# A hybrid encoder on one Trainium2 core: another order inside the block of seven products

## The chip, the cores and the metric

The kernel runs on one core of one Trainium2 chip. The metric is the device time of one execution in microseconds (us), and lower is better. The core has a matrix engine (TensorE, in the profile PE, with its weight loads as PEld), three engines for element work (VectorE or DVE, ScalarE or ACT, GpSimd or POOL) and a queue, SP, from which nearly all transfers between HBM and the core's memory are issued.

## The reference

Two layers work on 256 tokens of width 1024 in float32. Each has a token mixer and a gated MLP. The change touches the MLP alone:

```python
def _conv_ffn(xn, w_up, conv_w, conv_b, w_down):
    a, gval = jnp.split(xn @ w_up, 2, axis=-1)
    a = lax.conv_general_dilated(a, conv_w[:, None, :], ...,
                                 feature_group_count=D_FF) + conv_b
    return (jax.nn.gelu(a) * gval) @ w_down
```

D_FF is 2816, so `w_up` is 1024 x 5632 and `w_down` 2816 x 1024. The convolution takes each channel with its two neighbours in time.

## The kernel before

**Weights in pieces.** All weights stream through one object, `Weights`. A load (L174, on SP) brings 1 MB of float32 into a buffer `raw`; three such buffers take turns. (A load with a tag goes to a place of its own that is idle at the time.) Each load is used as two pieces, its halves 0 and 1. Each piece is split into two parts that TensorE takes at a higher rate: the high part `wh`, a copy by ScalarE (L255, here "the split"), and the low part `wl`, the remainder by VectorE (L257, "the rest"). Five pairs of `wh` and `wl` exist. A product then takes three matmuls for one of plain float32: x high by `wh`, x high by `wl`, x low by `wh`.

`get` (L278) hands the next piece to TensorE's code and, inside the MLP, splits the piece four further on. Behind that piece's rest comes whatever difference of weights `W.sums` holds for the piece (L224). Then `load` issues the loads that `ahead` (L148) names: as many as three untagged ones, from the earliest that is still needed by the piece just split and the two behind it.

**The order of the MLP is written by hand** (`manual_schedule`). Each piece has a place, counted from the start of the MLP, and the engines work in the order in which the code issues. `MLP_GROUPS` (L43) gives the groups: `a` and `g` with a number n are 512 columns of the convolved and of the gated half of `w_up`, four pieces of 12 matmuls each; `b` holds the last 256 columns of both halves; `w` is the block of seven products, which stands for columns group 3 of both halves; `d` are pieces of `w_down`, 12 matmuls each. a2 has places 16 to 19, g2 20 to 23, the block 24 to 45, b 46 to 49, a4 50 to 53, g4 54 to 57, and the rest are down pieces.

`at_place` (L1524) does what belongs to a place: the split of the piece four on (ACT), then whatever the place has "between" (VectorE's steps of a chunk, and the copies, additions and transposes that follow a finished group), then the rest of that piece (VectorE), then the matmuls, then what it has "behind". A finished group leaves TensorE's banks through two transposes on VectorE (L803), a write to HBM (L808) and four reads (L815), so that channels come to lie on partitions. This is called a crossing. The reads wait until the next load has been issued. All crossings of the MLP are transposed into one buffer, `crossing`.

**Chunk pairs.** The channels come in 22 chunks of 128, worked off in pairs f = 0, 2, ... 20. A pair has five steps (L1470): `fetch_up`, six scalings on ACT (L1486, L1488); `neighbours`, two additions on VectorE (L1492, L1493); `activate`, the gelu on ACT (L1496); `gate`, a multiplication on VectorE (L1500); and `keep_up`, a copy on ACT (L1508) and a subtraction on VectorE (L1509). `PAIR_PLACES` (L48) has two places p1 and p3 for each pair: `fetch_up` is behind p1, `neighbours` between and `activate` behind p1 + 1, `gate` between and `keep_up` behind p3. Chunks 8 and 9 need a2 and g2, chunks 12 to 15 the block, 16 to 19 a4 and g4, and 20 and 21 need b. Down piece k needs chunk k.

**The block** (L323 for the weights, L1550 for the products) computes two 512-column groups for even and odd tokens with seven products rather than eight. The weights' quadrants are "11" and "21" (upper and lower rows of the gated columns) and "12" and "22" (of the convolved ones). The products multiply "11", T1, "22", T2, "21", T3 and T4 by quadrants of x or by sums of them, where T1 = 12 - 11, T2 = 22 - T1, T3 = 22 - 12 and T4 = 21 - T2. Each difference is taken on VectorE in halves (L343), and each half is then split like any other piece. A half product has 6 matmuls. "11" and "12" are loaded to tagged places; "22" and "21" to `raw`. In before T1, T2 and T4 are written over "11" and T3 over "12".

`BLOCK` (L52) is the order of half products and down pieces ("d"), and `SUMS` (L57) says behind which piece each half of a difference is taken. The products share three banks: "11" and "21" one, T1 and "22" another, T2, T3 and T4 the third. Before a bank is added to further, its interim sum is taken out: "11" is copied to the third bank (L1592), T1 and "22" are copied out by ACT (L1596, L1599), and T2 and T3 are added to those copies by VectorE (L1603) and sent on their crossing.

Of the kernel before, what the change touches and what calls it, by code (L numbers as in the profile page):

```python
# [16 lines left out]
P = 128  # L17
# [28 lines left out]
)  # L46

PAIR_PLACES = (  # L48
    (11, 14), (14, 16), (19, 22), (21, 23), (46, 48), (49, 51), (52, 54), (58, 60), (61, 63), (64, 66), (66, 68),
)  # L50

BLOCK = (  # L52
    ("11", 0), ("11", 1), "d", ("T1", 0), ("T1", 1), "d", ("22", 0), ("22", 1), "d", ("T2", 0), ("T2", 1), "d",
    ("21", 0), ("21", 1), "d", ("T3", 0), ("T3", 1), "d", "d", ("T4", 0), ("T4", 1), "d",
)

SUMS = {  # L57
    ("11", 1): ("T1", 0), ("d", 0): ("T1", 1), ("22", 1): ("T2", 0), ("d", 2): ("T2", 1),
    ("T2", 0): ("T3", 0), ("T2", 1): ("T3", 1), ("21", 1): ("T4", 0), ("d", 4): ("T4", 1),
}  # L60
HALVES = (slice(0, 512), slice(512, D))
SEGMENTS = (HALVES, (slice(0, 512), slice(512, 768), slice(768, D)))

# [229 lines left out]
def encoder(ctx, tc, x, w_in, w_pool, pool_scale, w_a, w_b, w_o, norm1, norm2, w_up, conv_w,  # L293
            conv_b, w_down, rel_bias, norm_f, onehot, edges, out):
    nc = tc.nc
# [9 lines left out]
    W = Weights(tc, wpool, big, sm)  # L305

    def rows(w, r0, n=2, c0=0, width=1024, tag=None, pieces=2):

        src = w[r0 : r0 + n * P, c0 : c0 + width].rearrange("(k p) c -> p k c", p=P)
        h = n // pieces  # L310
        return W.add(
            src, (n, width), [((lambda t, j=j: t[:, j * h : (j + 1) * h, :]), (h, width)) for j in range(pieces)],
            tag,
        )
# [8 lines left out]
    def block(w, down, n):  # L323

        def quadrant(k, c0, tag=None):
            return rows(w, k * 512, 4, c0, 512, tag)

        gate, act = DFF + n * 512, n * 512
        made = {"11": quadrant(0, gate, "ybig"), "12": quadrant(0, act, "at2")}
        d = rows(down, 0)  # L330
        made["22"] = quadrant(1, act)
        d += rows(down, 2 * P)
        made["21"] = quadrant(1, gate)
        d += rows(down, 4 * P) + rows(down, 6 * P)
        home = {"T1": "11", "T2": "11", "T3": "12", "T4": "11"}
        of = {"T1": "12", "T2": "22", "T3": "22", "T4": "21"}

        def raw(name, j):
            return W.raw[made[name][0][0]][:, 2 * j : 2 * j + 2]

        def sum_of(name, j):
            at = raw(home[name], j)
            nc.vector.tensor_sub(out=at, in0=raw(of[name], j), in1=at)  # L343

        k = 0
        for unit in BLOCK:
            if unit == "d":
                key, piece = ("d", k), d[k]
                k += 1
            else:  # L350
                key = name, j = unit
                if name in home:
                    n0 = made["22"][0][0] if name == "T2" else d[k][0]
                    piece = (n0, lambda t, name=name, j=j: raw(home[name], j), (2, 512))
                else:
                    piece = made[name][j]
            if key in SUMS:
                W.sums[len(W.pieces)] = lambda name=SUMS[key]: sum_of(*name)
            W.use([piece])

    first_up = []
    for l in range(DEPTH):
# [8 lines left out]
        for kind, n in GROUPS:  # L371
            c0 = {"u": 0, "q": C_Q, "k": C_K}[kind] + n * 512
            pieces = rows(w_in[l], 0, 4, c0, 512)
            if (kind, n) in POOLS:
                g, at = POOLS[kind, n]
# [646 lines left out]
    for l in range(DEPTH):  # L1022
# [311 lines left out]
        with tc.manual_schedule():  # L1334
# [28 lines left out]
            for n, cc in enumerate(HALVES):  # L1363
# [14 lines left out]
                for t in range(2):  # L1378
                    nc.vector.scalar_tensor_tensor(
                        out=th[:, t], in0=th[:, t], scalar=1.0, in1=ps[t], op0=ALU.add, op1=ALU.mult  # L1380
# [12 lines left out]
            for i in range(4):  # L1393
                next(attended)
                if i >= 2:
                    made = first[i - 2][1]()
# [138 lines left out]
        def begin_values():  # L1535
# [7 lines left out]
        down = residual_mm(  # L1543
            lambda k: acts[k], NF, lambda *a: late["norm"].add(*a),
            fill=begin_values if l + 1 < DEPTH else None, whole=(l + 1 == DEPTH),
        )
# [130 lines left out]
```

## Time and profile before

| | us |
|---|---|
| median of 3 runs | 856.58 |
| lowest and highest of them | 855.93, 856.83 |
| the profiled execution as a whole | 859.7 |
| its span, first to last instruction | 857.9 |
| layer 1's block on TensorE | 312.50 to 356.07 |
| layer 2's block on TensorE | 734.55 to 778.73 |

Rows of a timeline give the start, the duration, the engine, the line and operation, what is written and read, how many instructions were merged, and in brackets how long the engine had been idle and what ended that. Durations overlap where instructions are pipelined, so the cost of an operation in a full queue is the distance from its start to the next one's. Rows of the chain of work that ended last give start, duration and what the end waited for. Rows by windows give, for a stretch, its length, the busy time of PE, PEld, DVE, ACT and POOL with the number of instructions, the clock granted to TensorE, the busy share of the DMA engines and GB/s.

### The profile page before, as it was taken

To read this page: it belongs to the slowest core of one execution; us is meant where nothing else is said; L and a number is where in the kernel's file an instruction comes from. 1 tells how busy PE (TensorE), PEld (TensorE's weight loads), DVE (VectorE), ACT (ScalarE), POOL (GpSimd) and SP (SyncE) were. 2 spreads that over 40 slices of the span, in tenths; PEclk is the share of its full clock that TensorE was granted. 3 is DMA by queue.
4 is the path that set the end of the run, shared out by engine and by line. 5 is a ranking of instruction groups with operands and counts; after the bars stand their busy time and mean duration, and the time that the engine had idled before them with its cause. 6 is when DMAs were issued, how large, how long until landed. Compare 5 with 4: busy or idle time off the path is not lost.

```text
span 857.9 us, 10949 instructions
## 1 busy us (share of the span) xinstructions
PE 841.6 (98%) x3901; PEld 700.7 (82%) x3901; DVE 646.1 (75%) x838; ACT 524.0 (61%) x757; POOL 35.6 (4%) x96
## 2 busy tenths in 40 slices
PE   9999999999999999999999999999999999899996
PEld 7888888888888887788788888888888888788885
DVE  6968777767767799787855787768577867987774
ACT  6744556654555775577745455577354657656784
POOL 1720000000010000000000000000000100000000
PEclk9999999999999999999999999999999999999998
DMA  8699986795748986798626889878776489758951
GB/s 300 210 309 306 299 283 226 263 294 210 249 163 291 284 289 214 234 325 281 239 99 221 263 280 322 247 228 266 247 260 240 147 271 322 265 197 280 333 171 50
DMA packets 147967, 214.03 MB, mean 249 GB/s; under 512 B 7800, under 2 KB 69184, under 8 KB 147912
## 3 DMA queue, kind: packets, MB, share of 16 engines
q1 hardware_dynamic: 147480, 212.67, 75.2%
q8 instruction: 31, 0.51, 0.2%
q10 hardware_dynamic: 432, 0.66, 0.2%
q14 instruction: 24, 0.20, 0.1%
HBM read 186.02 MB, written 27.28 MB: 249 GB/s over the span
## 4 chain that ended last, share of the span: by engine, by line
PE 79%; DVE 10%; DMA 7%; issue 2%; ACT 1%; SPq 1%; POOL 0%; ACTq 0%; DVEq 0%; POOLq 0%
PE t_ps L749 51%; PE v_ps L749 6%; DVE wl L257 5%; PE res_ps L667 5%; PE res_ps L668 5%; PE res_ps L666 5%; DMA raw<-in_w_down_dram 4%; PE v_ps L1002 3%; DMA crossing<-crossing 2%; DVE raw L343 2%; PE pool_ps L653 1%; PE v_ps L901 1%; DVE crossing L803 1%; PE o_ps L1285 1%; PE s_ps L1237 1%
## 5 line engine op out<-in xcount | busy, mean ns | idle before, releaser
L257 DVE TENSOR_TENSOR wl<-raw,wh 128x1024 fp32r<-128x1024 f32 x286 | 343.6, 1217 | 117.2 <-ACT wh L255 116.1
L255 ACT CAST wh<-raw 128x1024 fp32r<-128x1024 f32 x286 | 296.8, 1049 | 186.1 <-PE t_ps L749 98.4
L749 PE MATMUL t_ps<-wh,x 128*128 128x512 f32 x1280 | 399.8, 390 | 0.0
L749 PEld LDWEIGHTS t_ps<-wh,x 128*128 128x128 f32 x1280 | 240.3, 188 | 50.1
L749 PE MATMUL t_ps<-wl,x 128*128 128x512 f32 x640 | 249.0, 389 | 0.0
L749 PEld LDWEIGHTS t_ps<-wl,x 128*128 128x128 f32 x640 | 120.2, 188 | 24.7
L667 PE MATMUL res_ps<-wl,actq 128*128 128x512 f32 (+1 forms) x184 | 70.1, 381 | 1.1 <-DVE wl L257 1.1
L666 PE MATMUL res_ps<-wh,actq 128*128 128x512 f32 (+1 forms) x184 | 70.0, 380 | 0.0
L668 PE MATMUL res_ps<-wh,actk 128*128 128x512 f32 (+1 forms) x184 | 69.0, 380 | 0.0
L667 PEld LDWEIGHTS res_ps<-wl,actq 128*128 128x128 f32 x184 | 34.6, 188 | 8.5 <-DVE wl L257 1.9
L749 PE MATMUL t_ps<-wh,po 128*128 128x512 f32 x128 | 41.4, 395 | 0.0
L666 PEld LDWEIGHTS res_ps<-wh,actq 128*128 128x128 f32 x184 | 34.6, 188 | 6.7
L668 PEld LDWEIGHTS res_ps<-wh,actk 128*128 128x128 f32 x184 | 34.6, 188 | 6.5
L1488 ACT ACTIVATE a<-zga,prm 128x256 f32<-128x256 f32 x80 | 38.9, 513 | 0.0
L543 POOL TENSOR_SCALAR ss<-ss 128x1 f32<-128x1 f32 x8 | 2.3, 291 | 777.4 <-ACT junk L536 777.3
L803 DVE STREAM_TRANSPOSE crossing<-t_ps 128x512 f32<-128x512 f32 x36 | 23.9, 694 | 6.6 <-DMA crossing<-crossing 6.6
L749 PEld LDWEIGHTS t_ps<-wh,po 128*128 128x128 f32 x128 | 24.0, 188 | 4.9
L666 PE MATMUL res_ps<-wh,m 128*128 128x512 f32 (+1 forms) x72 | 26.5, 368 | 0.0
L667 PE MATMUL res_ps<-wl,m 128*128 128x512 f32 (+1 forms) x72 | 26.3, 365 | 0.0
L668 PE MATMUL res_ps<-wh,m 128*128 128x512 f32 (+1 forms) x72 | 26.0, 365 | 0.0
L749 PE MATMUL v_ps<-wh,x 128*128 128x512 f32 x80 | 25.7, 392 | 0.0
L749 PE MATMUL t_ps<-wl,po 128*128 128x512 f32 x64 | 24.9, 390 | 0.0
(211 smaller groups left out, 1045.5 us busy)
## 6 DMA issues: line engine op xcount, KB each, us to landing
raw<-in_w_in_dram SPq DMA_DIRECT2D x58, 1024.0 KB
raw<-in_w_up_dram SPq DMA_DIRECT2D x40, 1024.0 KB
raw<-in_w_down_dram SPq DMA_DIRECT2D x22, 1024.0 KB
crossing<-crossing SPq DMA_DIRECT2D x22, 512.0 KB
crossing<-way SPq DMA_DIRECT2D x16, 512.0 KB
raw<-in_w_a_dram SPq DMA_DIRECT2D x8, 1024.0 KB
raw<-in_w_o_dram SPq DMA_DIRECT2D x8, 1024.0 KB
zga<-crossing SPq DMA_DIRECT2D x40, 128.0 KB
```

Of the source, the lines that this page charges most:

```text
L255: inst = nc.scalar.copy(out=h, in_=src)
L257: inst = self.rests[i] = nc.vector.tensor_sub(out=l, in0=src, in1=h.bitcast(F32))
L343: nc.vector.tensor_sub(out=at, in0=raw(of[name], j), in1=at)
L653: nc.tensor.matmul(out, w(k), x, start=(steps is first and k == 0), stop=(steps is last and k == nk - 1), skip_group_check=turns["rest"],)
L666: nc.tensor.matmul(ps, ah, wh, start=first, stop=False, skip_group_check=on)
L667: nc.tensor.matmul(ps, ah, wl, start=False, stop=False, skip_group_check=on)
L668: nc.tensor.matmul(ps, al, wh, start=False, stop=last, skip_group_check=on)
L749: nc.tensor.matmul(ps, x2[:, 2 * n + j, part, t, :], w[:, j, :], start=(n + m == 0), stop=(n == last and m == 5),)
L803: nc.vector.transpose(out=y.rearrange("p q c j -> p c q j"), in_=rows)
L901: return nc.tensor.matmul(ps[t], a[:, k, t, :], w[:, k % 2, :], start=first, stop=last)
L1002: nc.tensor.matmul(ps[t], a[:, k, t, :], w[:, j, :], start=(k + m == 0), stop=(k == KD - 1 and m == 2),)
L1488: nc.scalar.mul(out=out, in_=a, mul=row(j, c))
```

## The change

- T1's two halves are taken behind the rests of the two pieces ahead of the block (g2's third and fourth). The halves of T2 are taken behind the rests of "22", T3's behind those of T2, T4's behind those of "21".
- T1, T2 and T4 are now written over "12", and T3, as T2 - 11, over "11". T3 no longer reads "22".
- Two down pieces stand ahead of "22" rather than one, and one ahead of T4 rather than two. The second down load is issued ahead of "22" and the third ahead of "21".
- The pairs from chunk 8 on have other places. Chunk 8's are 39 and 41, inside the block, rather than 46 and 48 behind it.

```diff
@@ -46,18 +46,15 @@
 )
 
 PAIR_PLACES = (
-    (11, 14), (14, 16), (19, 22), (21, 23), (46, 48), (49, 51), (52, 54), (58, 60), (61, 63), (64, 66), (66, 68),
+    (11, 14), (14, 16), (19, 22), (21, 23), (39, 41), (46, 48), (49, 51), (52, 54), (60, 62), (63, 65), (58, 60),
 )
 
 BLOCK = (
-    ("11", 0), ("11", 1), "d", ("T1", 0), ("T1", 1), "d", ("22", 0), ("22", 1), "d", ("T2", 0), ("T2", 1), "d",
-    ("21", 0), ("21", 1), "d", ("T3", 0), ("T3", 1), "d", "d", ("T4", 0), ("T4", 1), "d",
+    ("11", 0), ("11", 1), "d", ("T1", 0), ("T1", 1), "d", "d", ("22", 0), ("22", 1), "d", ("T2", 0), ("T2", 1), "d",
+    ("21", 0), ("21", 1), "d", ("T3", 0), ("T3", 1), "d", ("T4", 0), ("T4", 1), "d",
 )
 
-SUMS = {
-    ("11", 1): ("T1", 0), ("d", 0): ("T1", 1), ("22", 1): ("T2", 0), ("d", 2): ("T2", 1),
-    ("T2", 0): ("T3", 0), ("T2", 1): ("T3", 1), ("21", 1): ("T4", 0), ("d", 4): ("T4", 1),
-}
+SUMS = {"22": "T2", "T2": "T3", "21": "T4"}
 HALVES = (slice(0, 512), slice(512, D))
 SEGMENTS = (HALVES, (slice(0, 512), slice(512, 768), slice(768, D)))
 
@@ -327,36 +324,40 @@
 
         gate, act = DFF + n * 512, n * 512
         made = {"11": quadrant(0, gate, "ybig"), "12": quadrant(0, act, "at2")}
-        d = rows(down, 0)
+        d = rows(down, 0) + rows(down, 2 * P)
         made["22"] = quadrant(1, act)
-        d += rows(down, 2 * P)
+        d += rows(down, 4 * P)
         made["21"] = quadrant(1, gate)
-        d += rows(down, 4 * P) + rows(down, 6 * P)
-        home = {"T1": "11", "T2": "11", "T3": "12", "T4": "11"}
-        of = {"T1": "12", "T2": "22", "T3": "22", "T4": "21"}
+        d += rows(down, 6 * P)
+        made.update(T1=made["12"], T2=made["12"], T3=made["11"], T4=made["12"])
+        terms = {"T1": ("12", "11"), "T2": ("22", "12"), "T3": ("12", "11"), "T4": ("21", "12")}
 
         def raw(name, j):
             return W.raw[made[name][0][0]][:, 2 * j : 2 * j + 2]
 
-        def sum_of(name, j):
-            at = raw(home[name], j)
-            nc.vector.tensor_sub(out=at, in0=raw(of[name], j), in1=at)
-
+        def sum_later(i, name, j):
+
+            def make():
+                one, other = terms[name]
+                nc.vector.tensor_sub(out=raw(name, j), in0=raw(one, j), in1=raw(other, j))
+
+            W.sums[i] = make
+
+        for j in range(2):
+            sum_later(len(W.pieces) - 2 + j, "T1", j)
         k = 0
         for unit in BLOCK:
             if unit == "d":
-                key, piece = ("d", k), d[k]
+                W.use([d[k]])
                 k += 1
+                continue
+            name, j = unit
+            if name in SUMS:
+                sum_later(len(W.pieces), SUMS[name], j)
+            if name in terms:
+                W.use([(d[k][0], lambda t, name=name, j=j: raw(name, j), (2, 512))])
             else:
-                key = name, j = unit
-                if name in home:
-                    n0 = made["22"][0][0] if name == "T2" else d[k][0]
-                    piece = (n0, lambda t, name=name, j=j: raw(home[name], j), (2, 512))
-                else:
-                    piece = made[name][j]
-            if key in SUMS:
-                W.sums[len(W.pieces)] = lambda name=SUMS[key]: sum_of(*name)
-            W.use([piece])
+                W.use([made[name][j]])
 
     first_up = []
     for l in range(DEPTH):
```

## The prediction

> **What bounds the kernel now.** I read the cores view first, then the page, the chain of work that ended last, and the timelines of TensorE (PE), VectorE (DVE), ScalarE (ACT) and the SP queue through the block.
>
> ```profile
> core 0: 857.9 us, clock 0.997
> ```
> ```profile
> PE 841.6 (98%) x3901; PEld 700.7 (82%) x3901; DVE 646.1 (75%) x838; ACT 524.0 (61%) x757; POOL 35.6 (4%) x96
> ```
> ```profile
> 258.26 40.81 PE t_ps L749 x180
> ```
>
> TensorE is the bound, at full clock. The third line is from the chain: 180 matmuls without a gap in 40.81 us, 0.2267 us each. A block of seven products has just as many: 14 half products of 6 and 8 down pieces of 12. Without a wait it would take 40.8 us. The first PE rows of the block and of the piece behind it say what it does take, in layer 1 and layer 2:
>
> ```profile
> 312.50 0.39 PE L1578 MATMUL t_ps<-wh,x 128*128 128x512 f32 x1
> ...
> 356.07 0.39 PE L749 MATMUL t_ps<-wh,x 128*128 128x512 f32 x1
> ```
> ```profile
> 734.55 0.39 PE L1578 MATMUL t_ps<-wh,x 128*128 128x512 f32 x1
> ...
> 748.16 0.50 PE L1578 MATMUL t_ps<-wh,sx 128*128 128x512 f32 x1 [2.02 <-ACT kept L1596]
> ...
> 778.73 0.39 PE L749 MATMUL t_ps<-wh,x 128*128 128x512 f32 x1
> ```
>
> That is 43.57 and 44.18 us: 2.77 and 3.38 us lost, **6.15 us in all, the most that an edit inside the blocks can win**. The largest loss is the one shown: the third product ("22") opens on the bank that ScalarE still has to copy out (L1596), and that copy stands behind a split that waits for a difference.
>
> In the block the tight engine is VectorE. A half product is 6 × 0.2267 = 1.36 us on PE, but a half of a difference costs VectorE a rest (L257) and a subtraction (L343). Its rows around the entry of layer 1's block:
>
> ```profile
> 297.47 1.22 DVE L257 TENSOR_TENSOR wl<-raw,wh 128x1024 fp32r<-128x1024 f32 x1 [0.56 <-ACT wh L255]
> 300.19 1.23 DVE L257 TENSOR_TENSOR wl<-raw,wh 128x1024 fp32r<-128x1024 f32 x1 [1.50 <-ACT wh L255]
> 301.33 1.31 DVE L803 STREAM_TRANSPOSE crossing<-t_ps 128x512 f32<-128x512 f32 x2
> 302.56 0.65 DVE L1492 TENSOR_TENSOR y<-y,a 128x510 f32<-128x510 f32 x1
> 303.31 0.69 DVE L1493 TENSOR_TENSOR y<-y,a 128x510 f32<-128x510 f32 x1
> 303.96 1.23 DVE L257 TENSOR_TENSOR wl<-raw,wh 128x1024 fp32r<-128x1024 f32 x1
> 305.64 1.23 DVE L257 TENSOR_TENSOR wl<-raw,wh 128x1024 fp32r<-128x1024 f32 x1 [0.45 <-ACT wh L255]
> 307.37 1.23 DVE L343 TENSOR_TENSOR raw<-raw,raw 128x1024 f32<-128x1024 f32 x1 [0.51 <-DMA raw<-in_w_up_dram]
> ...
> 310.90 1.22 DVE L257 TENSOR_TENSOR wl<-raw,wh 128x1024 fp32r<-128x1024 f32 x1 [0.30 <-ACT wh L255]
> 312.04 1.22 DVE L343 TENSOR_TENSOR raw<-raw,raw 128x1024 f32<-128x1024 f32 x1
> 313.18 0.68 DVE L1509 TENSOR_TENSOR actk<-g,actq 128x512 fp32r<-128x512 f32 x1
> 313.78 0.68 DVE L1500 TENSOR_TENSOR g<-y,zg 128x512 f32<-128x512 f32 x1
> 314.38 1.22 DVE L257 TENSOR_TENSOR wl<-raw,wh 128x1024 fp32r<-128x1024 f32 x1
> ```
>
> From start to start: a rest 1.14 us, a difference 1.14, two transposes 1.23, a chunk pair's neighbours (L1492, L1493) 1.40, its keep (L1509) 0.60, its gate (L1500) 0.60. In program order the rows are the rests of g2's last two pieces (297.47 and 300.19), a2's transposes, neighbours of chunk 4, the rests of both halves of "11", and then T1's first difference at 307.37, which **waited 0.51 us for the load of quadrant "12"**. That load was issued late, behind others on SP:
>
> ```profile
> 298.94 0.40 SPq L174 DMA_DIRECT2D raw<-in_w_up_dram  x1
> ```
> ```profile
> 299.43 10.30 DMA raw<-in_w_down_dram
> ```
> ```profile
> 329.95 4.77 DMA raw<-in_w_down_dram
> ```
>
> It landed at about 307.3, 8.4 us after its issue. The next load, by the chain, was issued at 299.43 and landed at 309.73; the chain's shorter flight of a megabyte is 4.77 us.
>
> **The change part by part.**
>
> *T1's differences.* They move from behind the rests of "11" half 1 and down piece 0 to behind the rests of g2's last two pieces, three places earlier. Nothing in the diff issues "12" earlier: "11", "12" and the first down load are still issued once g2's first piece is split. So VectorE, which takes its queue in order, reaches the difference at 297.47 + 1.22 = 298.7 and stands there until 307.37: **8.7 us of waiting where 0.5 was**. Queued behind it are the rest at 300.19 and all rows up to 305.64; ACT waits behind them for the neighbours, PE for the rests. That work cost nothing before, under the flight of "12"; now it is behind it. Layer 2 has the same picture, with "12" landing just ahead of
>
> ```profile
> 730.65 1.22 DVE L343 TENSOR_TENSOR raw<-raw,raw 128x1024 f32<-128x1024 f32 x1 [0.61 <-DMA raw<-in_w_up_dram]
> ```
>
> 3.90 us ahead of PE's entry (734.55), where layer 1 has 5.13. Call the start of this first difference L. I count VectorE from L to the rest of T1's second half, the piece that PE reaches soonest relative to its rest. Two differences and six rests: 8 × 1.14 = 9.12; two pairs of transposes (a2, g2) 2.46; two neighbours 2.80; two gates and two keeps 2.40: 16.8 us. To that come two handoffs through ACT, from these rows:
>
> ```profile
> 304.04 0.64 ACT L1496 ACTIVATE y<-y 128x512 f32<-128x512 f32 x1
> 304.57 1.03 ACT L255 CAST wh<-raw 128x1024 fp32r<-128x1024 f32 x1
> 305.51 0.52 ACT L1488 ACTIVATE a<-zga,prm 128x256 f32<-128x256 f32 x1
> ...
> 307.74 0.51 ACT L1488 ACTIVATE a<-zga,prm 128x256 f32<-128x256 f32 x1
> ```
>
> Chunk 4's activation (0.53) follows its neighbours, the split of "11" half 1 (0.94) follows that, and chunk 6's six scalings (305.51 to 308.25, 2.74) follow that. These 4.2 us and VectorE's return (0.1) stand against 2 × 1.14 of rests and a gate of 0.60 that VectorE can do meanwhile: 1.4 us more, and 0.1 until the last rest is written. So that rest ends at L + 18.3 = 325.7. PE, unhindered, would want it at 312.50 + 3 × 1.36 + 2.72 + 0.23 = 319.5: **PE is 6.1 us late here in layer 1, and 7.4 in layer 2**.
>
> *Down pieces 1 and 2 ahead of "22".* PE then has 5.4 us rather than 2.7 between T1 and the bank that L1596 empties, so that wait goes; I count its gain within the sum. In return T3 and T4, which share a bank, have one down piece between them rather than two, so T4 must wait for VectorE's addition of T3 (L1603). "22", no longer read by T3's difference, frees its buffer a little earlier, which nothing in this sum waits for.
>
> *The loads' order on SP.* The second down load goes out where "22" did, and "22" one place later, behind a2's crossing, whose transposes now end at L + 3.4 + 1.2 = 312.0. With 4.8 us of flight it lands at 317; its split is wanted after T1's and d1's, past 325. That cover of 8 us hides it, and d1's rest frees the third down load's buffer at L + 19.4 = 326.8, to land at 331.6, with its split wanted past 336.
>
> *Chunk 8's steps into the block* (39, 41 for 46, 48): neighbours, gate and keep, 2.60 us, now stand on VectorE ahead of that addition. At 46 they were hidden. From the rest of T1's second half to the end of T3's addition VectorE has 17 rests (19.38), six differences (6.84), the first addition and transpose and the second addition, by
>
> ```profile
> 346.31 0.68 DVE L1603 TENSOR_TENSOR kept<-t_ps,kept 128x512 f32<-128x512 f32 x1
> 347.03 0.71 DVE L803 STREAM_TRANSPOSE crossing<-kept 128x512 f32<-128x512 f32 x1
> 351.52 0.72 DVE L803 STREAM_TRANSPOSE crossing<-t_ps 128x512 f32<-128x512 f32 x1 [3.79 <-DMA crossing<-crossing]
> 352.16 4.59 DVE L257 TENSOR_TENSOR wl<-raw,wh 128x1024 fp32r<-128x1024 f32 x4
> ```
>
> 0.72 + 0.64 + 0.72 = 2.08, and the 2.60: 30.9 us. **T4 can start at L + 18.3 + 30.9 = L + 49.2**: 356.6 in layer 1 and 779.9 in layer 2. PE, 6.1 and 7.4 late, would be there at 354.0 and 777.3 (312.50 or 734.55, plus 12 × 1.36 + 7 × 2.72 = 35.36): a second wait of some 2.5 us. T4 and the last down piece add 5.44: the blocks end at 362.0 and 785.3, against 356.07 and 778.73: **5.9 + 6.6 us**.
>
> *The first piece of b.* Its rest now stands behind T3's addition, a transpose, the 3.79 us for the crossing (the buffer of the two transposes is one) and another transpose, which in before delayed the last down piece. 356.6 + 0.64 + 3.8 + 0.64 + 1.2 = 362.9 against 362.2 needed (one matmul into the piece): **0.7 us** in each layer.
>
> *The other chunks* (10 to 20 at other places) lie where PE has no gap and ACT and DVE have room:
>
> ```profile
> 400.00:410.00 10.00, 10.00 (x45) 8.26 (x45) 7.68 (x11) 9.34 (x16) 0.00 (x0) 1.00 0.83 309
> ```
>
> Cost between 0 and, if ACT's 0.66 us of room were all used up, about 1 us a layer; gain at most nothing, since nothing waits. I take 0.
>
> **Sum:** 5.9 + 6.6 + 2 × 0.7 = 13.9 us on the profiled span: 871.8 for 857.9. That execution took 859.7 as a whole, 3.1 above the median of 856.58; I add the difference to the median: **870.5 us**.
>
> Two costs no row shows. *When "12" lands* with VectorE standing still: not before its issue plus the shortest flight, 298.94 + 4.77 = 303.7, so L is up to 3.7 us earlier and the whole up to 7.4 lower, 863.1; I stay by 307.37, as nothing ahead of it in the queue changes. *Quadrant "21"*: it can be loaded only when d3's rest frees its buffer, about L + 26.3, and its split is wanted 4.6 us later. A flight of 4.77 just serves; one of 8.4, as that of "12", would idle VectorE for 3.8 us more a layer, 878.1 in all. DMA is light there, so I go by the short one.
>
> **The rivals.**
>
> 1. *The flight of "12" shrinks* (863 to 867). For it: later loads and a2's write compete less. Against: the load behind it landed 2.4 us later, as if each had its turn. The Trainium skill ("DMA: Bandwidth & Descriptors", Queues, rings and completion order) says that each DMA engine consumes descriptors in ring order, but that completion isn't first in, first out; by that rule later loads take nothing from "12"'s start, and this rival would be worth little.
> 2. *"21" or another late load adds a third wait* (874 to 878), with the bound worked out above.
> 3. *The other side, faster:* the load of "12" isn't what the difference meets, and only the two waits that the edit removes count. If VectorE reached the difference with "12" there, T4 could start at 298.7 + 49.2 = 347.9, the unhindered 347.86, plus some 1.5 us of VectorE's waits for splits: 42.3 + 0.7 us for the block and its follower where 43.57 were. With the same lead in layer 2 its 44.18 become 43.0 too: 1.8 us off the two, 854.8. It turns from loss to gain where "12" lands at 307.37 - 6.6 = 300.8, 1.8 us after its issue; the shortest flight is 4.77. I see no way to it but a misread order of the queues.
> 4. *The clock falls in the new waits.* The row with layer 2's 2.02 us wait shows full clock (the 1.00):
>
> ```profile
> 740.00:750.00 10.00, 7.76 (x33) 5.88 (x33) 10.00 (x11) 6.44 (x9) 0.00 (x0) 1.00 0.79 234
> ```
>
> A fall before T4 is swallowed by T4's wait; at half clock through T4 it costs 12 × 0.2267 = 2.7 us a layer: 876. The Trainium skill ("TensorE: Matmul & The Clock Gate", What's actually happening) has the clock halved after an idle window of about 3.4 us. By that rule none of my waits, 2 to 3 us each, would do it, though one somewhat longer would.
>
> **How the numbers follow.** My forecast (867 to 874): 0.62. Rival 1: 0.13. Rival 2: 0.13. Rival 3: 0.06, of which 0.04 beyond 0.2%. Rival 4: 0.06. The range goes from rival 1's lowest, 863.1, less 1.1 should the waits at b shrink with it, to the bound of "21", 878; outside it are rival 3 and what I have not thought of, which I put at 0.15 to 0.2 together. Slower by over 0.2% (1.7 us, about what a measurement can tell from no change): 0.62 + 0.13 + 0.13 + 0.06 = 0.94; faster 0.04; same 0.02.
>
> **What would show it.** Right: in the waits, "DVE raw <- DMA" grows from 1.1 to some 17 us in two waits of 8 to 9; the rest of g2's last piece starts at 308.5 rather than 300.2; PE waits at "11", at down piece 0 and at T1 for rests, and at T4 for L1603; the wait for L1596 is gone. Wrong: if the first difference waits little, rival 3 stands; if PE is late at T1 but not at T4, the count of chunk 8 is too high; if ACT waits for a load of w_up at "21", it is rival 2.

## The result and the profile after

The change makes the kernel slower: **863.16 us** against 856.25 us for the kernel before on the same chip (medians; 862.88 to 865.09 and 855.29 to 856.83), a ratio of 1.0087 with a 95% interval of 1.0069 to 1.0104. The prediction was 870.5 with a range of 862 to 878: the right side, inside the range, about twice the size.

The profiled execution took 863.14 us, close to its kernel's median, while that of before (859.7) stood 3.4 us above its own. The profiles therefore differ by only 3.4 us of span where the medians differ by 6.9. Sums below are made on the spans, as in the prediction, and sizes of single edits come from medians. Lines after L254 are those of before moved by a few: L252 is the split, L254 the rest, L342 a difference, L750 a matmul of an ordinary group, L1579 one of the block, L1597 the copies of banks, L1604 the addition of T3 (and T2).

The cores view of the changed kernel:

```profile
core 0: 861.3 us, clock 0.997
```

The timeline of TensorE, layer 1 and then layer 2 (from 737.83). In each the first row opens the block and the last is the first matmul of the piece behind it; of the rows between, those with the waits at down piece 0 (layer 1) and at T4 are shown.

```profile
312.11 0.39 PE L1579 MATMUL t_ps<-wh,x 128*128 128x512 f32 x1
...
316.40 0.50 PE L667 MATMUL res_ps<-wh,actq 128*128 128x512 f32 x1 [0.87 <-ACT wh L252]
...
317.73 0.50 PE L668 MATMUL res_ps<-wl,actq 128*128 128x512 f32 x1 [0.82 <-DVE wl L254]
...
353.72 0.77 PE L1579 MATMUL t_ps<-wh,x 128*128 128x512 f32 x1 [2.08 <-DVE kept L1604]
...
360.83 0.39 PE L750 MATMUL t_ps<-wh,x 128*128 128x512 f32 x1
...
737.83 0.39 PE L1579 MATMUL t_ps<-wh,x 128*128 128x512 f32 x1
...
778.49 0.47 PE L1579 MATMUL t_ps<-wh,x 128*128 128x512 f32 x1 [2.08 <-DVE kept L1604]
...
784.05 0.39 PE L750 MATMUL t_ps<-wh,x 128*128 128x512 f32 x1
```

The blocks take 48.72 and 46.22 us, where before took 43.57 and 44.18: 5.15 and 2.04 more. The wait for the copy L1597 is gone in both layers, and T4 has a wait of 2.08 us for L1604 in both. (Left out above are a wait of 0.86 us at T1 in layer 1 and three of 0.46, 0.83 and 0.87 in layer 2.) What comes behind the blocks became shorter, which the prediction did not have.

VectorE's timeline around the entry of layer 1 and ahead of T4, and at the entry of layer 2:

```profile
305.10 1.23 DVE L342 TENSOR_TENSOR raw<-raw,raw 128x1024 f32<-128x1024 f32 x1 [6.80 <-DMA raw<-in_w_up_dram]
306.25 1.22 DVE L254 TENSOR_TENSOR wl<-raw,wh 128x1024 fp32r<-128x1024 f32 x1
...
352.89 0.68 DVE L1604 TENSOR_TENSOR kept<-t_ps,kept 128x512 f32<-128x512 f32 x1
...
729.88 1.22 DVE L342 TENSOR_TENSOR raw<-raw,raw 128x1024 f32<-128x1024 f32 x1 [5.86 <-DMA raw<-in_w_up_dram]
```

SP's timeline shows when quadrant "12" (`w_up`) was issued, in layer 1 and in layer 2:

```profile
298.29 0.40 SPq L171 DMA_DIRECT2D raw<-in_w_up_dram  x1
...
723.99 0.39 SPq L171 DMA_DIRECT2D raw<-in_w_up_dram  x1
```

T1's first difference stood 6.80 and 5.86 us for the load, and everything queued behind it on VectorE moved with it: the rest of g2's last piece starts at 306.25. But "12" landed 6.8 and 5.9 us after its issue, where before's rows gave 8.4 and 8.0.

One thing the timeline above shows that no wait explains: from 353.72 to the block's end T4 and one down piece took 7.11 us in layer 1, and 5.56 in layer 2 (778.49 to 784.05). The windows of the changed kernel behind the two waits give the clock granted to TensorE (the number ahead of the last two):

```profile
354.00:355.00 1.00, 1.00 (x3) 0.81 (x3) 0.32 (x1) 0.00 (x0) 0.00 (x0) 0.50 0.00 0
...
356.00:357.00 1.00, 1.00 (x4) 0.81 (x3) 0.00 (x0) 0.34 (x1) 0.00 (x0) 0.50 0.98 262
...
779.00:780.00 1.00, 1.00 (x6) 0.80 (x5) 0.09 (x1) 0.00 (x0) 0.00 (x0) 1.00 0.00 0
```

In layer 1 the clock was halved in all three windows from 354 to 357; in layer 2, after a wait of the same length, it was not.

### The profile page after: what moved, and what is told of

Its sections match the earlier page's. It is cut to its first block, busy times and chain, and to the rows that moved or that the text cites. A ratio compares the mean times of both kernels' runs of the same rounds, so it can differ in the third digit from the quotient of the medians.

```text
span 861.3 us, 10959 instructions
## 1 busy us (share of the span) xinstructions
PE 845.2 (98%) x3901; PEld 702.3 (82%) x3901; DVE 645.2 (75%) x838; ACT 522.6 (61%) x757; POOL 35.1 (4%) x96
## 4 chain that ended last, share of the span: by engine, by line
PE 80%; DVE 10%; DMA 5%; ACT 2%; issue 2%; SPq 0%; POOL 0%; ACTq 0%; DVEq 0%; POOLq 0%
PE t_ps L750 50%; PE v_ps L750 6%; DVE wl L254 5%; PE res_ps L668 5%; PE res_ps L667 5%; PE res_ps L669 5%; DMA raw<-in_w_up_dram 3%; PE v_ps L1003 3%; DVE raw L342 2%; PE pool_ps L654 1%; PE v_ps L902 1%; DMA crossing<-crossing 1%; PE t_ps L1579 1%; PE o_ps L1286 1%; PE s_ps L1238 1%
## 5 line engine op out<-in xcount | busy, mean ns | idle before, releaser
L254 DVE TENSOR_TENSOR wl<-raw,wh 128x1024 fp32r<-128x1024 f32 x286 | 343.8, 1217 | 109.5 <-ACT wh L252 108.6
L750 PE MATMUL t_ps<-wh,x 128*128 128x512 f32 x1280 | 399.5, 390 | 0.0
L252 ACT CAST wh<-raw 128x1024 fp32r<-128x1024 f32 x286 | 296.0, 1048 | 169.5 <-PE t_ps L750 103.0
L750 PEld LDWEIGHTS t_ps<-wh,x 128*128 128x128 f32 x1280 | 240.3, 188 | 49.8
L750 PE MATMUL t_ps<-wl,x 128*128 128x512 f32 x640 | 249.1, 389 | 0.0
L750 PEld LDWEIGHTS t_ps<-wl,x 128*128 128x128 f32 x640 | 120.2, 188 | 25.1 <-DVE wl L254 0.2
L750 PE MATMUL t_ps<-wh,po 128*128 128x512 f32 x128 | 41.4, 395 | 0.0
L342 DVE TENSOR_TENSOR raw<-raw,raw 128x1024 f32<-128x1024 f32 x16 | 19.5, 1217 | 12.7 <-DMA raw<-in_w_up_dram 12.7
L750 PEld LDWEIGHTS t_ps<-wh,po 128*128 128x128 f32 x128 | 24.0, 188 | 4.9
L1497 ACT ACTIVATE y<-y 128x512 f32<-128x512 f32 x22 | 13.9, 633 | 21.3 <-DVE y L1494 21.3
```

Of the source, the lines that this page charges most:

```text
L252: inst = nc.scalar.copy(out=h, in_=src)
L254: inst = self.rests[i] = nc.vector.tensor_sub(out=l, in0=src, in1=h.bitcast(F32))
L342: nc.vector.tensor_sub(out=raw(name, j), in0=raw(one, j), in1=raw(other, j))
L750: nc.tensor.matmul(ps, x2[:, 2 * n + j, part, t, :], w[:, j, :], start=(n + m == 0), stop=(n == last and m == 5),)
L1497: nc.scalar.activation(t["y"], t["y"], AF.Gelu_apprx_tanh)
```

## The experiments

Medians are compared with those of the kernel before, measured beside them on the same chip. The medians of before run from 855.90 to 857.17, so a difference between two rows with different ones is uncertain by about 1 us. The blocks' lengths and the stretch from layer 1's block end to the first value product of layer 2 are read from TensorE's timeline of each profile.

| kernel | median us | before | ratio (95%) | block 1 | block 2 | behind block 1 |
|---|---|---|---|---|---|---|
| before | | | | 43.57 | 44.18 | 73.65 |
| changed | 863.16 | 856.25 | 1.0087 (1.0069 to 1.0104) | 48.72 | 46.22 | 72.16 |
| late_t1 | 852.87 | 856.71 | 0.9960 (0.9944 to 0.9975) | 41.98 | 43.44 | 72.45 |
| late_chunk8 | 857.78 | 856.71 | 1.0014 (0.9995 to 1.0033) | 44.91 | 44.32 | 72.49 |
| late_both | 849.88 | 856.71 | 0.9913 (0.9890 to 0.9936) | 40.80 | 40.95 | 72.16 |
| tail_only | 851.96 | 856.71 | 0.9940 (0.9918 to 0.9962) | 42.39 | 43.62 | 72.15 |
| pair20_only | 860.62 | 855.90 | 1.0050 (1.0033 to 1.0067) | 42.70 | 41.61 | 73.29 |
| others_only | 856.73 | 855.90 | 1.0005 (0.9995 to 1.0015) | 42.50 | 41.48 | 73.65 |
| old_order | 849.80 | 855.90 | 0.9920 (0.9908 to 0.9933) | 40.80 | 40.80 | 72.16 |
| pair20_clean | 853.48 | 857.17 | 0.9955 (0.9939 to 0.9971) | 42.73 | 44.16 | 72.16 |
| tail_hand68 | 852.11 | 857.17 | 0.9944 (0.9924 to 0.9964) | 42.66 | 41.61 | 71.90 |
| early_old_loads | 861.26 | 857.17 | 1.0040 (1.0022 to 1.0058) | 48.37 | 45.40 | 72.14 |

The last column falls into two groups, with one kernel (pair20_only) beside them: about 73.65, and about 72.15. That is the trail to the part of the result that was not foreseen.

**late_t1: the changed kernel with T1's differences behind "11" half 1 and down piece 0, as in before.**

```diff
-            sum_later(len(W.pieces) - 2 + j, "T1", j)
+            sum_later(len(W.pieces) + 1 + j, "T1", j)
```

> The changed kernel with T1's two differences back behind the rest of "11" half 1 and behind that of down piece 0; all else as changed. My theory: the wait for quadrant "12" (6.8 and 5.9 us in the changed kernel) goes to under 1 us, PE has no wait at "11", down piece 0 and T1 (3.8 and 2.8 us late there), but chunk 8 and T3's addition still hold T4 up by 1 to 2.6 us a layer. Blocks of 42 to 43.4 us for 48.7 and 46.2: about 855 (853 to 857). Rival, that what costs is the order inside the block or chunk 8: little changes, 861 to 863.

It took 852.87, just below the expected 853 to 857: the early differences cost 10.3 us of the changed kernel's time (863.16 - 852.87). No wait at "11", down piece 0 or T1 is left; TensorE's only waits in the blocks are these two, in the two layers:

```profile
348.52 0.47 PE L1579 MATMUL t_ps<-wh,x 128*128 128x512 f32 x1 [0.91 <-DVE kept L1604]
...
769.21 0.47 PE L1579 MATMUL t_ps<-wh,x 128*128 128x512 f32 x1 [2.09 <-DVE kept L1604]
```

They are at T4, for the addition that chunk 8's steps delay. The theory that the two terms are separate edits with separate waits holds.

**late_chunk8: the changed kernel with chunk 8 behind the block.** Chunks 10, 12 and 14 follow it one slot later each.

```diff
-    (11, 14), (14, 16), (19, 22), (21, 23), (39, 41), (46, 48), (49, 51), (52, 54), (60, 62), (63, 65), (58, 60),
+    (11, 14), (14, 16), (19, 22), (21, 23), (46, 48), (49, 51), (52, 54), (55, 57), (60, 62), (63, 65), (58, 60),
```

> The changed kernel with chunk 8's steps back at 46 and 48 (10, 12 and 14 follow at 49, 52, 55; 16, 18 and 20 as changed); T1's differences stay early. My theory: the wait of 6 to 7 us for "12" stays, and with it PE's 3 to 4 us at the entry; T4's wait of 2.1 us, and the half clock behind it in layer 1, go. Blocks of about 44.6 and 43.7: 857 to 858. Rival, that T4's wait comes from the single down piece ahead of it and not from chunk 8: T4 still waits over 1 us, 860 to 862.

It took 857.78: chunk 8 in the block cost 5.4 us. T4 waits in neither layer, and the wait for "12" stays (6.48 us in layer 1, 6.31 in layer 2). The second of TensorE's first two waits in layer 1, 1.3 us behind the one of 0.85, and a window behind them:

```profile
317.85 0.50 PE L668 MATMUL res_ps<-wl,actq 128*128 128x512 f32 x1 [0.84 <-DVE wl L254]
```
```profile
320.00:322.00 2.00, 2.00 (x6) 1.51 (x5) 2.00 (x5) 2.00 (x3) 0.00 (x0) 0.50 0.00 0
```

Two waits of 0.85 and 0.84 us were enough here: at 320 to 322 the granted clock was 0.50. The changed kernel had the same two (0.87 and 0.82) at the same place without it, so a part of each of these differences is the clock and not the wait.

**late_both: both edits together.**

```diff
-    (11, 14), (14, 16), (19, 22), (21, 23), (39, 41), (46, 48), (49, 51), (52, 54), (60, 62), (63, 65), (58, 60),
+    (11, 14), (14, 16), (19, 22), (21, 23), (46, 48), (49, 51), (52, 54), (55, 57), (60, 62), (63, 65), (58, 60),
...
-            sum_later(len(W.pieces) - 2 + j, "T1", j)
+            sum_later(len(W.pieces) + 1 + j, "T1", j)
```

> The changed kernel with both undone, T1's differences and chunk 8; what is left is the order of the down pieces, T3 as T2 - 11, and chunks 14 to 20 earlier. My theory: no wait of over 0.5 us in the blocks, 41 us each, which is 2.5 and 3.2 us better than before: about 850.5, and 847 if the earlier chunks also shorten the ends of the layers by the 1.5 and 1.9 us by which the two profiles differ there. Rival, that the order itself costs (T4 waits with one down piece ahead): 855 to 857.

849.88 us: **0.9913 of before (0.9890 to 0.9936)**, faster than both kernels. Its blocks take 40.80 and 40.95 us, which is what 180 matmuls take without a wait. So early T1 and chunk 8 cost the changed kernel 13.3 us together (863.16 - 849.88). Added singly to late_both they cost 7.9 (late_chunk8) and 3.0 (late_t1), 2.4 less than together; the clock that fell behind T4's wait, which of these kernels only the two together showed, is a candidate for that, with 1.67 us in layer 1. And the rest of the change gains 6.8 us (856.71 - 849.88). The next experiments ask where it lies.

**tail_only: the kernel before with the last four pairs at the places of late_both.**

```diff
-    ... (46, 48), (49, 51), (52, 54), (58, 60), (61, 63), (64, 66), (66, 68),
+    ... (46, 48), (49, 51), (52, 54), (55, 57), (60, 62), (63, 65), (58, 60),
```

> The kernel before with only the last four chunk pairs at other places (14 at 55, 16 at 60, 18 at 63, 20 at 58). From the end of the block to the end of the layer the changed kernel's profile is 1.5 and 1.9 us shorter than that of before. If the places do that: 852.5 to 853.5. If it is a difference of the two executions (the profiled one of before took 3.4 us more than its median): 856 to 857, no change.

851.96 us, 4.75 below before and half a microsecond below the 852.5 to 853.5 expected: most of the gain is here.

**others_only: of the four, only chunks 14, 16 and 18.**

```diff
-    ... (52, 54), (58, 60), (61, 63), (64, 66), (66, 68),
+    ... (52, 54), (55, 57), (60, 62), (63, 65), (66, 68),
```

> The kernel before with pairs 14, 16 and 18 at the places of the four moved pairs, but pair 20 left at 66 and 68. My theory (pair 20 alone matters): no change, 856 to 857. Rival, that the pairs 14 to 18 do it: 852 to 853.5.

No gain: 856.73, ratio 1.0005, and the stretch behind block 1 is before's 73.65.

The code of its blocks is that of before, and yet its profile (span 853.7) is 4.2 us shorter than that of before (857.9); 3.8 of them lie in the two blocks. Before's third product waited 2.02 us for the copy L1596 in layer 2, and 1.22 in layer 1; the row of layer 1, and then the same two waits in this kernel:

```profile
324.77 0.50 PE L1578 MATMUL t_ps<-wh,sx 128*128 128x512 f32 x1 [1.22 <-ACT kept L1596]
```
```profile
323.35 0.50 PE L1578 MATMUL t_ps<-wh,sx 128*128 128x512 f32 x1 [0.24 <-ACT kept L1596]
...
744.34 0.50 PE L1578 MATMUL t_ps<-wh,sx 128*128 128x512 f32 x1 [0.23 <-ACT kept L1596]
```

VectorE reached T1's first difference 5.71 us ahead of the block in both layers and found "12" there. The same holds throughout: six profiles have this block, twelve blocks in all. In the four of them in which the difference waited for "12" (both of before, layer 2 of tail_only and of pair20_clean) the wait for the copy is 1.22 to 2.04 us, in the other eight 0.23 or 0.24. So the profile of before shows an execution in which "12" came late. The 6.15 us that the prediction took from it as the most to be won inside the blocks are 2.4 in others_only (42.50 and 41.48, less 40.80 each).

**pair20_only: only the pair of chunks 20 and 21, at 55 and 57.** At these places it overwrites chunk 8's activations before down piece 8 has used them, so the output is another.

```diff
-    ... (58, 60), (61, 63), (64, 66), (66, 68),
+    ... (58, 60), (61, 63), (64, 66), (55, 57),
```

> The kernel before with only chunk pair 20 at another place (55 and 57 rather than 66 and 68). My theory: in before the last down pieces of all four output segments wait for chunk 20's keep (it ends at 843.7 in layer 2), so the segments end together and the norm's work stands behind them in one row; with pair 20 early they end one by one. The whole gain of the four moved pairs (851.96 for 856.71): 852 to 853. Rival, that the pairs 14 to 18 do it: 855.5 to 857 here.

860.62, slower than before, with 73.29 us behind block 1. It misses what was expected, and since the conflict over the storage comes with it, nothing can be read from it on the pair's place. The test was therefore made again at places without the conflict:

**pair20_clean: only that pair, at 58 and 60.**

```diff
-    ... (58, 60), (61, 63), (64, 66), (66, 68),
+    ... (58, 60), (61, 63), (64, 66), (58, 60),
```

> The kernel before with only the pair of chunks 20 and 21 at places 58 and 60 rather than 66 and 68. Theory (this pair alone makes the end of the MLP shorter, as its keep and its share of VectorE no longer lie among the additions of the last segments): the stretch from the block's end to the next layer's first value product falls from 73.65 to about 72.15 us in layer 1, what follows the last matmul of layer 2 falls from 8.4 to 6.4, and the time to 852 to 853 where the kernel before takes about 856.3. Rival (the four pairs together are needed): 855.5 to 857.

853.48, ratio 0.9955 (0.9939 to 0.9971), and 72.16 us behind block 1: this pair alone does it. (The time is 0.5 us above the 852 to 853 expected, beside a before 0.9 above the 856.3 assumed there.) VectorE's timeline at the end of layer 1, in before and then in pair20_clean: the last keep of the layer, and the additions to the residual (L558), one for each finished bank:

```profile
421.21 0.68 DVE L1509 TENSOR_TENSOR actk<-g,actq 128x512 fp32r<-128x512 f32 x1
...
423.45 0.69 DVE L558 TENSOR_TENSOR h<-res_ps,h 128x512 f32<-128x512 f32 x1 [0.41 <-PE res_ps L668]
...
424.36 0.69 DVE L558 TENSOR_TENSOR h<-res_ps,h 128x512 f32<-128x512 f32 x1 [0.22 <-PE res_ps L668]
```
```profile
416.07 0.69 DVE L1509 TENSOR_TENSOR actk<-g,actq 128x512 fp32r<-128x512 f32 x1
...
420.45 0.69 DVE L558 TENSOR_TENSOR h<-res_ps,h 128x512 f32<-128x512 f32 x1 [1.42 <-PE res_ps L668]
...
423.33 0.68 DVE L558 TENSOR_TENSOR h<-res_ps,h 128x512 f32<-128x512 f32 x1
```

TensorE's timeline, the first transpose of the next norm in before and in pair20_clean:

```profile
427.43 0.44 PE L578 MATMUL xt_ps<-ident,xn 128*128 128x128 f32 x2 [1.73 <-DVE xn L569]
```
```profile
426.40 0.44 PE L578 MATMUL xt_ps<-ident,xn 128*128 128x128 f32 x2 [0.26 <-DVE xn L569]
```

In before the layer's last keep is at 421.21, 65.1 us behind the block's end; in pair20_clean it is 59.6 behind it (416.07; block end 356.52). With the late keep TensorE goes through the high parts (`actq`) of the last banks first and comes back for the low parts (`actk`, which the keep writes): in before's timeline the six full-width rows from 420.70 to 421.86 are all of high parts, and the low parts follow from 422.32, once the keep is done (of its rows, the last of the six and the first of the low parts):

```profile
421.86 0.39 PE L667 MATMUL res_ps<-wl,actq 128*128 128x512 f32 x1
...
422.32 0.40 PE L668 MATMUL res_ps<-wh,actk 128*128 128x512 f32 x1
```

TensorE doesn't idle at that, but the banks finish in a bunch: the additions stand 0.91 us apart, where pair20_clean has 2.88. The norm's sums then follow the bunch late, and TensorE waits 1.73 us for it where pair20_clean waits 0.26. That the place of this pair makes the difference is shown by the edit; that it does so through the bunch is read from these rows. In layer 2 nothing covers the same delay: from the last residual matmul to the end of the span it is 8.4 us in before and 6.4 in the changed kernel.

**tail_hand68: tail_only with the order by hand kept up to place 68.** When the last pair leaves off at place 65 rather than 68, the order by hand ends earlier, too. That was a rival cause.

```diff
-                    if not between and not behind:
+                    if place > 68:
                         break
```

> tail_only with the order by hand kept up to place 68, where the kernel before has its end, rather than up to 65, where tail_only's last pair leaves off. Theory (the gain of 4 to 5 us comes from where chunk 20's steps stand): as tail_only, 851.5 to 853. Rival (it comes from the order by hand ending three places earlier, so that the last additions and the scheduler's own order start sooner): 855.5 to 857, with the wait before the transposes of the norm back at about 1.7 us.

852.11, as tail_only. It is where the steps stand, not where the order by hand ends.

**old_order: late_both with the half products, down pieces and loads in the order of before.** What is left of the change inside the block is where the differences of T2 and T4 are taken, what T3 is made from, and what the differences are written over. (T3's are behind the pieces of T2 in both kernels.)

```diff
-    ("11", 0), ("11", 1), "d", ("T1", 0), ("T1", 1), "d", "d", ("22", 0), ("22", 1), "d", ("T2", 0), ("T2", 1), "d",
-    ("21", 0), ("21", 1), "d", ("T3", 0), ("T3", 1), "d", ("T4", 0), ("T4", 1), "d",
+    ("11", 0), ("11", 1), "d", ("T1", 0), ("T1", 1), "d", ("22", 0), ("22", 1), "d", ("T2", 0), ("T2", 1), "d",
+    ("21", 0), ("21", 1), "d", ("T3", 0), ("T3", 1), "d", "d", ("T4", 0), ("T4", 1), "d",
...
-        d = rows(down, 0) + rows(down, 2 * P)
+        d = rows(down, 0)
...
-        d += rows(down, 4 * P)
+        d += rows(down, 2 * P)
...
-        d += rows(down, 6 * P)
+        d += rows(down, 4 * P) + rows(down, 6 * P)
```

> The kernel with T1's differences and chunk 8 late (849.88), but with the down pieces and the loads in the order of before: one down piece ahead of "22", two ahead of T4. My theory: the wait of "22" for the copy of T1 out of its bank (L1596) is back with some 1 to 2 us a layer, 851.5 to 852.5, as in the kernel with only the last chunks moved. Rival, that the 2.1 us between those two come from T3 no longer reading "22" and from the sums' places: 849.5 to 850.5.

The expectation fell: 849.80, as late_both, and both blocks take 40.80 us without a wait. With T1 late, the second down piece ahead of "22" is worth nothing. The waits of before at L1596 went with the other treatment of the differences; their places and what they are written over were not tried apart. The places of the last pairs are the same in tail_only and old_order, and the medians are 2.2 us apart, beside different ones of before. Of the blocks' step from 42.39 and 43.62 us to 40.80 twice, a part isn't the edit's: in layer 2 of tail_only the difference met "12" late, in old_order it did not. tail_hand68, which has the same block as tail_only and that wait in neither layer, takes 42.66 and 41.61, which makes 1.9 and 0.8 us for the edit.

**early_old_loads: old_order with T1's differences early.** It asks why "12" flew for a shorter time than in before.

```diff
-            sum_later(len(W.pieces) + 1 + j, "T1", j)
+            sum_later(len(W.pieces) - 2 + j, "T1", j)
```

> old_order (places of late_both, block and loads in the order of before) with T1's differences early, so late_chunk8 with the loads' old order: behind quadrant 12 go one down load and quadrant 22 rather than two down loads. Theory A (the order of the loads set how long 12 flew): its flight is 8.0 to 8.4 us as in before, where late_chunk8 has 6.3, VectorE waits 1.5 to 2 us longer in each layer, 860 to 862. Theory B (what shortened the flight is that a2's crossing is no longer written behind it, as its transposes stand behind the wait): flight about 6.3, time as late_chunk8, 857 to 859.

SP's timeline and VectorE's, in layer 1 and layer 2:

```profile
299.93 0.40 SPq L171 DMA_DIRECT2D raw<-in_w_up_dram  x1
...
723.52 0.39 SPq L171 DMA_DIRECT2D raw<-in_w_up_dram  x1
```
```profile
306.31 1.23 DVE L342 TENSOR_TENSOR raw<-raw,raw 128x1024 f32<-128x1024 f32 x1 [6.93 <-DMA raw<-in_w_up_dram]
...
729.76 1.23 DVE L342 TENSOR_TENSOR raw<-raw,raw 128x1024 f32<-128x1024 f32 x1 [6.20 <-DMA raw<-in_w_up_dram]
```

The flight is 6.4 and 6.2 us, as in late_chunk8 (6.3 and 6.3), and so, by one execution of each, the order of the loads is not what shortened it. The time missed both expectations in part: 861.26 lies in the band given for the other theory, 3.5 us above late_chunk8. A row of TensorE in layer 1 shows a part of the reason:

```profile
329.26 0.50 PE L1579 MATMUL t_ps<-wh,sx 128*128 128x512 f32 x1 [0.49 <-ACT kept L1597]
```

With T1 early and one down piece ahead of "22", the wait for the bank (L1597) is back: 0.49 us here and 0.90 in layer 2, whose block is 1.08 longer than in late_chunk8. So the two down pieces, worth nothing in old_order, have a use where T1's rests come late. Layer 1's block is 3.46 longer: besides the 0.49, TensorE waited 0.81 for the last down piece's rest, and L had a lead of 5.74 us on its entry (312.05) where late_chunk8 has 7.33, which makes 1.6. The flights being equal, that is the issue of "12", which came later relative to TensorE. Some 0.6 of the 3.46 are not accounted for.

**again: the changed kernel once more, one execution.**

> The changed kernel once more, for its profile: whether TensorE's clock falls to half again behind T4's wait of 2.1 us in layer 1 (it did in the first profile, and not in layer 2 with as long a wait). If the fall goes with the length of the wait alone, it is there again in layer 1 or in both; if it goes with when the wait falls, either may be.

This execution took 869.68 us, 6.5 above the median; 1.9 of that lie ahead of layer 1's block. VectorE's waits for "12" and TensorE's start of T4, each in layer 1 and layer 2:

```profile
307.87 1.22 DVE L342 TENSOR_TENSOR raw<-raw,raw 128x1024 f32<-128x1024 f32 x1 [7.05 <-DMA raw<-in_w_up_dram]
...
734.91 1.23 DVE L342 TENSOR_TENSOR raw<-raw,raw 128x1024 f32<-128x1024 f32 x1 [8.06 <-DMA raw<-in_w_up_dram]
```
```profile
356.48 0.47 PE L1579 MATMUL t_ps<-wh,x 128*128 128x512 f32 x1 [2.08 <-DVE kept L1604]
...
783.53 0.47 PE L1579 MATMUL t_ps<-wh,x 128*128 128x512 f32 x1 [2.07 <-DVE kept L1604]
```

The blocks begin at 314.00 and 740.66, 6.13 and 5.75 us behind L, not 7.01 and 7.95, and take 49.65 and 50.02 us, not 48.72 and 46.22. T4 starts at L + 48.61 and L + 48.62, to 0.01 us as in the other profile of this kernel. So in one and the same kernel the landing of "12" moves from one execution to another, and the blocks' ends with it. (Whether the two ran on the same chip is not known.) In layer 1 it is the issue that moved: "12" was issued 12.36 us ahead of the block, not 13.82, and its flight was 6.2 us, not 6.8. In layer 2 both moved. The clock fell behind T4's wait in both layers here (0.50 in the windows 358 to 360 and 785 to 787), and T4 and the down piece took 7.17 and 7.15 us.

## Why the prediction was right, and where it was not

**The two costs it named are the costs.** T1's differences wait for "12" and hold up VectorE, and chunk 8's steps delay T3's addition, for which T4 waits. late_t1, late_chunk8 and late_both remove them singly and together.

**The count of VectorE's work held.** T4 was to start at L + 49.2; it started at L + 48.62 in layer 1 (353.72 - 305.10), L + 48.61 in layer 2 (778.49 - 729.88), and at the same in the second profile. T4's wait was to be some 2.5 us and was 2.08.

**The step that was mis-sized: when "12" lands, seen from TensorE's entry.** The prediction kept L at 307.37 and the leads of 5.13 and 3.90 us. They became 7.01 (312.11 - 305.10) and 7.95 (737.83 - 729.88): 1.9 and 4.05 us of delay that did not come. TensorE came to T4 4.2 us late in layer 1 (353.72 - 2.08 - 312.11 - 35.36) and 3.2 in layer 2; the predicted 6.1 and 7.4, less these differences, are 4.2 and 3.35. The waits for "12" came to 12.7 us in all (6.80 + 5.86) where some 17 were named as the sign. The sentence that failed is "I stay by 307.37, as nothing ahead of it in the queue changes". Nothing ahead of it had to change: the 307.37 was itself that of an execution in which "12" came late (see others_only). 3.75 us of the 5.95 came from shorter flights (8.43 to 6.81, 8.02 to 5.89) and 2.2 from an earlier issue relative to TensorE's entry. So rival 1, the shorter flight, came true in this profile, and the time lies in its 863 to 867. That it lies there is partly luck: by the lead alone it would be 864.5 (870.5 - 5.95), and the terms below, of both signs, are in it too. The single execution of the second profile, with leads of 6.13 and 5.75, came to 869.68, near the forecast: the term varies by itself, and the forecast took one value of it for fixed. That nearness is luck as well: the fallen clock, which the forecast put at nothing, cost 1.7 us in each layer there and made up for the 3.4 us at the ends of the layers, which it did not have either.

The prediction set the Trainium skill's rule ("DMA: Bandwidth & Descriptors", Queues, rings and completion order) against that rival: descriptors are taken in ring order. From that it concluded that later loads take nothing from "12"'s start. The order of the loads behind it indeed made no difference in early_old_loads. But the flights differed: 5.9 to 6.8 us in the profiles of the changed kernel, late_chunk8 and early_old_loads, 6.2 and 7.4 in the second profile of the changed kernel, and 8.4 and 8.0 (before), 9.2 (tail_only), 7.7 (pair20_clean), 7.6 (late_t1) and 6.5 us (late_both, the last four in layer 2) in those profiles of late T1 where the difference met its load. The two groups overlap, and one kernel gave different flights in two executions. Nor are they of one kind: in the other twelve blocks with T1 late the difference came 8.1 to 8.2 us after the issue of "12" and found it there, and how short those flights were no row shows. The second group is therefore mostly of loads that came late, and doesn't show that an early T1 shortens the flight. What sets it is left open. With T1 early, a2's crossing is written only after "12" has landed, which would explain it, but in layer 2 of late_both that crossing was issued 1.8 us behind "12" and the flight was 6.5 all the same.

**The step that failed: "The other chunks ... gain at most nothing, since nothing waits."** The pair of chunk 20 at 58 rather than 66 is worth 3.7 us by itself (853.48 against 857.17), and tail_only 4.75. The prediction read the window 400 to 410, where TensorE is indeed full. It didn't read the end of the layer, where before's row at 427.43 shows 1.73 us of waiting, nor the last 8.4 us of the span.

**"That wait goes" by the two down pieces: right, for this kernel.** old_order shows the wait go without them, but its T1 is late. With T1 early, as here, and one down piece ahead of "22" the wait is there, 0.49 and 0.90 us (early_old_loads); with two it is not (late_chunk8 and the changed kernel).

**Rival 2 gave its sign and no cost.** The sign was to be that ACT waits for a load of `w_up` at "21". In layer 2 it did, 2.83 us until 759.98. But VectorE stood for nothing there: its rows start at 758.99 and 760.13, a full distance of 1.14 us, and T4 starts at L + 48.6 as in layer 1. The sign should have been looked for in VectorE's rows.

**0.7 us at b's first piece, twice:** no wait shows there. 1.4 us too much.

**Rival 4, the clock, was half right.** It was priced at 2.7 us a layer. In layer 1 of the profile T4 and the down piece took 1.67 us more than the 5.44 of full clock, in layer 2 0.12. The Trainium skill ("TensorE: Matmul & The Clock Gate", What's actually happening) gives about 3.4 us as the idle window, and the prediction took from it that waits of 2 to 3 us would do nothing. The runs differ: 2.08 us did it, and in late_chunk8 two of 0.85 with a matmul between. The same section calls the window free-running, and with that the traces agree: the same wait did it in one layer and not in the other.

The sum on the spans: 13.9 predicted, 3.4 measured. Of the 10.5 between them, 5.95 are the lead, 1.2 the count to T4 (twice 0.6), 1.4 b's first piece, 3.4 the ends of the layers (1.49 behind block 1, 1.92 behind block 2), 0.4 an entry that layer 1 reached earlier; the clock took 1.8 back (1.67 and 0.12). That leaves 10.55. By the medians the shortfall is 7.0, since the profiled execution of before was itself 3.4 above its median. others_only shows where such an execution loses that: in the blocks, where "12" comes late.

## What to carry to other kernels

An operation that must wait for a load costs what stands behind it in its engine's queue, so place it by when the load lands and not by when its operands could be used; the same work, three places later, was worth 10 us here. Before writing "nothing waits" for a step that moves, read every place at which its results are used, above all the end of a layer and the end of the program: a late last operand can leave the bound engine busy and still make it finish everything at once. And where a transfer's landing sets the sum, take its flight as a range: its ends here were 5.9 and 9.2 us for the same megabyte. What one profile of the kernel before loses is such a value too: 6.15 us in the blocks of one execution, 2.4 in another with the same blocks.

## What the runs showed of the hardware that was not expected

TensorE's granted clock fell to 0.50, for about 3.4 us in layer 1 of the changed kernel (rows of half pace from 353.72 to 357.21), after waits far shorter than that: after 2.08 us there and in both layers of its second profile, after 0.85 and 0.84 us in late_chunk8, and after 1.15, 0.90 and 0.82 us in early_old_loads (both in layer 1). Behind waits of the same lengths it stayed at 1.00 in layer 2 of the changed kernel and of late_t1 (2.09 us). The three falls behind T4's wait, one in the first profile of the changed kernel and two in the second, cost 1.7 us each: T4 and the down piece took 7.11, 7.17 and 7.15 us, where full clock gives 5.44.

A load of 1 MB landed 5.9 to 9.2 us after its issue at one and the same place of the program.
